# A two-layer hybrid trunk on one core: the first norm as products with a diagonal, and the mixers' modulation pieces loaded earlier

## The chip, the core and the metric

One core of one Trainium2 chip. TensorE (PE) multiplies, VectorE (DVE), ScalarE (ACT) and GpSimd (POOL) work on tiles of 128 partitions, SyncE (SP) issues the loads. The time is the device time of one launch in microseconds; the profile is of one execution. A granted clock of 1.0 is PE at 2.4 GHz, 0.5 is 1.2 GHz.

## The reference

Two layers over 256 tokens of width 1024 in fp32. `mod` is the conditioning of each layer; its six pieces of 1024 shift, scale and gate the two halves of the layer.

```python
def hybrid_layer(x, c, ada_w, ada_b, ...):
    mod = jax.nn.silu(c) @ ada_w + ada_b
    sh_m, sc_m, gt_m, sh_f, sc_f, gt_f = jnp.split(mod, 6)
    h = rms_norm(x, g_pre_mix) * (1.0 + sc_m) + sh_m
    rq, rk, rv, rg, lx, ly, fq, fk, fv, ff, gates = split(h @ w_in)
    y_ret = silu(rg) * head_norm(retention(rope(rq), rope(rk), rv))
    y_lru = gelu(ly) * rg_lru(causal_conv(lx), ...)
    y_fox = forgetting_attention(fq, fk, fv, log_sigmoid(ff + b_f))
    g = sigmoid(gates)
    merged = g[0] * (y_ret @ ret_w_o) + g[1] * (y_lru @ lru_w_o) + g[2] * (y_fox @ fox_w_o)
    x = x + gt_m * rms_norm(merged @ w_out, g_post_mix)
    h = rms_norm(x, g_pre_mlp) * (1.0 + sc_f) + sh_f
    return x + gt_f * rms_norm(square(relu(h @ w1)) @ w2, g_post_mlp)
```

## The kernel before

Every fp32 operand of a large product is split in two: a high half, which ACT casts to the reduced type (line 241), and a low half, which DVE forms as the difference (line 242). A product is then three matmuls (`mm3`, lines 364 to 366): high by high, low by high, high by low. The weights come as 512 KB halves, two for a column block of 256, into `wraw`, a ring of five buffers; SP issues each load when a buffer is free. The split halves stand in `wpair`, four buffers, which are two items. An item is one column block: 48 matmuls of 256 columns into one of two PSUM buffers (`ps`), which DVE and ACT empty: lines 914 (`fql`, low half of the attention's queries), 678 (`fvl`, `fkl`, `yrl`), 872 and 875 (gates and merge).

`mix_order` lists the items of a mixer in the order in which they are computed. In layer 0 the 53 are: 11 for gates and the recurrence's input (`g0`, `lx`, `g1`, `lru`), then `rg` x4, `g1`, `w_r` x4, `g1`, `ly` x4, `fq`, `w_l` x4, `fv` x4, `fq` x3, `fk` x4, `g2` x4, `w_f` x4, `w_o` x4. Layer 1 has 61 with the same 42 at the end.

`weight_order` makes one list, `ORDER`, of all loads. Between the items it puts the modulation's pieces ("ada"): 12 pieces in layer 0's mixer and 8 in layer 1's, spread evenly from the item that is `MIXR[l][0]` items before the mixer's end to the one `MIXR[l][1]` before it. A piece is two loads of 512 KB into `wraw` and, on DVE, two sums `ada_sum` of 128x1024 with the silu of c (`sir`, line 296) and one small addition (line 292); it frees its buffer when the sum is done. `prefetch` walks the list two or three items ahead of the one that PE computes, and each engine works through its own queue in order. `side` puts the pieces of the recurrence, the rotations and the attention between the items by a budget in us per item (`BUDGET`).

The first projection (`first_rows`) is another order. It takes the eight rows k of 128 channels one after the other. A row has four tiles of 512 KB in the pool `wfirst`, later `wraw`: the pieces sc_m and sh_m of that row, the weights of rv, and those of rq and rk. DVE sums the first two, ACT makes the scale `a` and shift `sh` of the row (lines 494, 495), then `hh` (line 513) and its fp32 twin `hf` (line 514), DVE the low half `hl`. PE multiplies the row into all rv, rq and rk banks at once. Before that the rows of x are squared (ACT, line 445), the inverse root comes from POOL (lines 199, 200), DVE scales x to `xn` (line 466), PE transposes it (line 450), ACT copies it to `xr` (line 468). `silu_rows` spreads the silu of c over the partitions (lines 283 to 289).

Of the kernel before, what the change touches and what calls it, by code (L numbers as in the profile page):

```python
# [10 lines left out]
F32 = mybir.dt.float32  # L11
# [22 lines left out]
P = 128  # L34
D = 1024
# [51 lines left out]
    return name in ('rv', 'w_o', 'w2') or (name == 'w1' and cix < 4)  # L87


MIXR = ((22, 8), (20, 8))  # L90
MLPR = ((5, 28), (5, 15))


# [25 lines left out]
def trunk_kernel(ctx, tc, x, c, vec, con, ffw, wts, out):  # L119
# [21 lines left out]
    nc.sync.dma_start(csb[:, :P], con[:, :P])  # L141
    for t in range(2):
        nc.sync.dma_start(xs[:, t, :], x[t])
    nc.sync.dma_start(vsb, vec)

    def cn(name):
        o, w = CON[name]
# [87 lines left out]
    def split_tiles(broad, n=C):  # L235
        return halves_of(wp.tile([P, 2 * D + SLOT_PAD], F32R, name="wpair", tag="wpair", bufs=NHL), broad, PHASE * broad, n)

    def split(t, hi, lo):
        if hi.shape[1] == 2:
            t = t.rearrange("p (k j) c -> p k (j c)", k=2)  # L240
        A.copy(hi, t)  # L241
        V.tensor_tensor(lo, t, hi.bitcast(F32), ALU.subtract)  # L242

    early = []
# [32 lines left out]

    mods = {l: cpool.tile([P, 48], F32, name=f"mod{l}") for l in range(L)}

    def silu_rows():  # L280

        th = sp.tile([P, KD], F32, name="cth", bufs=1)
        A.activation(th, ccol, AF.Tanh, scale=0.5)
        V.scalar_tensor_tensor(th, th, 1.0, ccol, ALU.add, ALU.mult)
        for j, copy in ((0, A.copy), (1, V.tensor_copy)):
            ps = pa.tile([P, 4, P], F32, name="crp", tag="a")
            for k in range(4):
                T.transpose(ps[:, k, :], th[:, 4 * j + k:4 * j + k + 1].to_broadcast([P, P]), ident)
            copy(sir[:, j * 512:(j + 1) * 512], ps.rearrange("p k c -> p (k c)"))

    def mod_bias(l, o, n, src):
        V.tensor_tensor(mods[l][:, o:o + n], src, vc(l, 'ada_b')[:, o:o + n], ALU.add)
# [162 lines left out]
    def first_rows():  # L455


        silu_rows()
        xn = U("T6", [P, 2, D], F32, "xn")
        xr = U("T7", [P, KD, S], F32, "xr")  # L460

        def norm(t):
            ss = sp.tile([P, 1], F32, name="ss1")
            square_sum(xs[:, t, :], ss)
            r = rstd_of(ss, eps)
            V.tensor_scalar(xn[:, t, :], xs[:, t, :], r, None, ALU.mult)
            for k0 in (0, 4):
                transposed(xn[:, t, :], k0, lambda pt, k0: A.copy(xr[:, k0:k0 + 4, t * P:(t + 1) * P], pt))

        one = sp.tile([P, KD], F32, name="one_sc")  # L470
        V.scalar_tensor_tensor(one, vc(0, 'ada_b')[:, 8 * PARTS['sc_m']:8 * PARTS['sc_m'] + 8], 1.0, vc(0, 'pre_mix'),
                               ALU.add, ALU.mult)
        a, sh = mod(0, 'sc_m'), mod(0, 'sh_m')
        hh, hl = new_h()
        raws = []

        def load(n):
            while len(raws) < min(n, 2 * KD):
                home = FIRST[len(raws)]
                if home:  # L480
                    t = U(home, [P, 2, KH * C], F32, "wfirst")
                    for j in range(2):
                        nc.sync.dma_start(t[:, j, :], wts[pos[0], j])
                    raws.append([t[:, j, :].rearrange("p (k c) -> p k c", k=KH) for j in range(2)])
                else:
                    raws.append([raw_half(j) for j in range(2)])
                pos[0] += 1

        def sums(k):
            kc, o = slice(k, k + 1), 8 * PARTS['sh_m'] + k  # L490
            m = sp.tile([P, 2], F32, name="mrow")
            for j in range(2):
                ada_sum(raws[2 * k][j], m[:, j:j + 1])
            A.activation(a[:, kc], m[:, 0:1], AF.Identity, bias=one[:, kc], scale=vc(0, 'pre_mix')[:, kc])
            A.activation(sh[:, kc], m[:, 1:2], AF.Identity, bias=vc(0, 'ada_b')[:, o:o + 1])

        def halves(k, j):
            hi, lo = split_tiles(not j)
            split(raws[2 * k + 1][j], hi, lo)
            return hi, lo  # L500

        load(FIRST_AHEAD)
        norm(0)
        norm(1)
        sums(0)
        rv = [[pool.tile([P, 2, C], F32, name="rvp", tag=tag) for pool, tag in ((pg, "g"), (pz, "z"))]
              for t in range(2)]
        qk = [[pa.tile([P, 2, S], F32, name="qkp", tag="a") for i in range(2)] for j in range(2)]
        for k in range(KD):
            load(2 * k + FIRST_AHEAD + 2)  # L510
            kc, f = slice(k, k + 1), tmp("t1", "hf")[:, 0, :]
            wh, wl = halves(k, 0)
            A.activation(hh[:, k, :], xr[:, k, :], AF.Identity, bias=sh[:, kc], scale=a[:, kc])
            A.activation(f, xr[:, k, :], AF.Identity, bias=sh[:, kc], scale=a[:, kc])
            V.tensor_tensor(hl[:, k, :], f, hh[:, k, :].bitcast(F32), ALU.subtract)
            for j in range(2):
                for t in range(2):
                    tk = slice(t * P, (t + 1) * P)
                    mm3(rv[t][j].rearrange("p h c -> p (h c)"), hh[:, k, tk], hl[:, k, tk], wh[:, j, :], wl[:, j, :],
                        k == 0, k == KD - 1)  # L520
            if k + 1 < KD:
                sums(k + 1)
            wh, wl = halves(k, 1)
            if k == KD - 1:
                nc.sync.dma_start(csb[:, P:5 * P], con[:, P:5 * P])
                early.extend(raw_half(j) for j in range(2))
                nc.sync.dma_start(csb[:, 5 * P:], con[:, 5 * P:])
            for j in range(2):
                for i in range(2):
                    for m in range(2):  # L530
                        n, cs = 2 * j + i, slice(m * P, (m + 1) * P)
                        mm3(qk[j][i][:, m, :], wh[:, n, cs], wl[:, n, cs], hh[:, k, :], hl[:, k, :], k == 0 and m == 0,
                            k == KD - 1 and m == 1, skip_group_check=True)
        return (hh, hl), rv, qk
# [129 lines left out]
    def mixer(l, nm, h=None, rvp=None, qkp=None):  # L664
# [333 lines left out]
        for n, i in mix_order(l):  # L998
# [5 lines left out]
            elif n in ('g0', 'g1', 'g2'):  # L1004
                gate_evac(int(n[1]), i)
            elif n == 'lx':
                if (l, i) == (0, 0):
                    lru_consts()
                conv(i)
            elif n == 'lru':  # L1010
                for h in heads[:NH_R]:
                    finish(h)
                wl.append(weight(l, 'lru', 0))
                gs = [Side(lru_gates(j)) for j in range(4)]
            elif n == 'rg':
                if i == 0:
                    finish(heads[-1])
                    yr = U("T1", [P, KD, S], F32R, "yrh"), U("T2", [P, KD, S], F32R, "yrl")
                ret_gate(i, yr)
            elif n == 'w_r':  # L1020
                if i == 0:
                    rec = Side(recurrence(), *gs)
                merge(0, 'w_r', i, yr)
            elif n == 'ly':
                if i == 0:
                    finish(rec)
                    yl = U("T3", [P, KD, S], F32R, "ylh"), U("T4", [P, KD, S], F32R, "yll")
                gelu_gate(i, yl)
            elif n == 'w_l':
                merge(1, 'w_l', i, yl)  # L1030
            elif n == 'fq':
                if (l, i) == (0, 0):
                    V.tensor_tensor(both, ident[:, 0:NH_F], ident[:, CUM_LO:CUM_LO + NH_F], ALU.add)
                    A.mul(sel, both, -1.0)
                if i == 0:
                    fq = U("T1", [P, NH_F, S], F32R, "fqh"), U("T2", [P, NH_F, S], F32R, "fql")
                fox_q(i, *fq)
            elif n == 'fv':
                if i == 0:
                    fv = U("T3", [P, 2, D], F32R, "fvh"), U("T4", [P, 2, D], F32R, "fvl")  # L1040
                fox_v(i, *fv)
            elif n == 'fk':
                if i == 0:
                    fk = U("T5", [P, NH_F, S], F32R, "fkh", True), U("T6", [P, NH_F, S], F32R, "fkl", True)
                    yf = U("T7", [P, KD, S], F32R, "yfh"), U("T8", [P, KD, S], F32R, "yfl")
                fox_k(i, *fk)
            elif n == 'w_f':
                if i == 0:
                    side()
                    mh, ml = U("T1", [P, KD, S], F32R, "mh"), U("T2", [P, KD, S], F32R, "ml")  # L1050
                    nm = Norms(l, 'm', (l, 'f'), ("T3", "T4", "T7"))
# [168 lines left out]
```

## Time and profile before

| | us |
|---|---|
| three runs, median (lowest, highest) | 1125.44 (1123.99, 1126.6) |
| the profiled execution | 1126.98 |
| its span in the trace | 1125.2 |
| PE busy | 1096.8 (97%) |
| DVE busy | 870.1 (77%) |
| ACT busy | 617.5 (55%) |

Busy time is a sum over all stages. Where PE stands still is read from the table of its waits and from windows laid over single stages, and why, from the timeline of the engine it waits for.

### The profile page before, as it was taken

Reading aid. Unit: us, or ns where it says so; the run is one execution under the profiler, and the core shown is the slowest. Engines: PE = TensorE matmul, PEld = TensorE weight load, DVE = VectorE, ACT = ScalarE, POOL = GpSimd, SP = SyncE. Lnnn points to the kernel's source line nnn. Section 1 sums busy time; section 2 is a strip of 40 time slices with the busy share of each in tenths; the row PEclk is TensorE's granted clock in tenths of the full one; section 3 lists DMA queues with packets and bytes.
Section 4 is the critical chain, followed back from the end, with each engine's and each line's share of the span. In section 5 each row is a group of like instructions: output and inputs, shape, how many; then the busy total and the mean of one; then the engine's idle time right before and its main releaser. Section 6 shows DMA issues by size and latency. Waiting matters only on the chain.

```text
span 1125.2 us, 20478 instructions
## 1 busy us (share of the span) xinstructions
PE 1096.8 (97%) x8164; PEld 1034.8 (92%) x8164; DVE 870.1 (77%) x1324; ACT 617.5 (55%) x924; POOL 43.7 (4%) x60
## 2 busy tenths in 40 slices
PE   6999999999999999999999999999999999999997
PEld 5999999998899889989879999999999997989986
DVE  6998788878887789888586768887868788866543
ACT  6676695544455645444455658755434655645441
POOL 0001000000000210000030010000000002000000
PEclk9999999999999999999999999999999999999999
DMA  9954646679876569998845465566777584875641
GB/s 359 408 179 155 197 136 216 193 248 314 282 249 220 193 214 323 332 327 295 299 140 185 151 194 162 185 207 194 235 248 265 193 290 133 283 269 197 195 159 59
DMA packets 74284, 255.43 MB, mean 227 GB/s; under 512 B 10108, under 2 KB 12492, under 8 KB 74188
## 3 DMA queue, kind: packets, MB, share of 16 engines
q1 hardware_dynamic: 74188, 254.12, 67.2%
q8 instruction: 64, 1.05, 0.4%
q14 instruction: 32, 0.26, 0.1%
HBM read 253.00 MB, written 1.09 MB: 226 GB/s over the span
## 4 chain that ended last, share of the span: by engine, by line
PE 75%; DVE 9%; DMA 8%; issue 4%; ACT 3%; POOL 1%; DVEq 0%; POOLq 0%; SPq 0%; ACTq 0%
PE ps L366 22%; PE ps L365 22%; PE ps L364 22%; DMA wraw<-in_wts_dram 7%; DVE wpair L242 3%; DVE wraw L296 1%; ACT wpair L241 1%; ACT junk L445 1%; PE rvp L364 1%; PE rvp L365 1%; PE rvp L366 1%; POOL rs_v L199 1%; PE qkp L365 1%; PE qkp L364 1%; PE qkp L366 1%
## 5 line engine op out<-in xcount | busy, mean ns | idle before, releaser
L242 DVE TENSOR_TENSOR wpair<-wraw,wpair 128x1024 fp32r<-128x1024 f32 (+1 forms) x286 | 347.3, 1220 | 74.1 <-ACT wpair L241 72.7
L241 ACT CAST wpair<-wraw 128x1024 fp32r<-128x1024 f32 (+1 forms) x286 | 298.3, 1049 | 191.4 <-PE ps L366 122.5
L364 PE MATMUL ps<-hh,wpair 128*128 128x256 f32 x1312 | 364.9, 278 | 5.3 <-DVE fvl L678 2.8
L366 PE MATMUL ps<-hh,wpair 128*128 128x256 f32 x1312 | 363.4, 277 | 0.1
L365 PE MATMUL ps<-hl,wpair 128*128 128x256 f32 x1312 | 363.1, 277 | 0.0
L364 PEld LDWEIGHTS ps<-hh,wpair 128*128 128x128 f32 x1312 | 246.8, 188 | 6.5 <-DVE fvl L678 3.2
L366 PEld LDWEIGHTS ps<-hh,wpair 128*128 128x128 f32 x1312 | 246.5, 188 | 0.4 <-DVE wpair L242 0.3
L365 PEld LDWEIGHTS ps<-hl,wpair 128*128 128x128 f32 x1312 | 246.6, 188 | 0.2
L296 DVE SCALAR_TENSOR_TENSOR wraw<-wraw,sir 128x1024 f32<-128x1024 f32 x82 | 100.0, 1222 | 44.9 <-DMA wraw<-in_wts_dram 44.6
L241 ACT CAST wown<-wraw 128x1024 fp32r<-128x1024 f32 x72 | 74.7, 1048 | 62.4 <-DMA wraw<-in_wts_dram 40.6
L242 DVE TENSOR_TENSOR wown<-wraw,wown 128x1024 fp32r<-128x1024 f32 x72 | 87.4, 1222 | 26.2 <-ACT wown L241 25.9
L364 PE MATMUL ps<-wpair,mih 128*128 128x512 f32 x144 | 56.3, 391 | 0.0
L365 PE MATMUL ps<-wpair,mih 128*128 128x512 f32 x144 | 56.1, 389 | 0.0
L366 PE MATMUL ps<-wpair,mil 128*128 128x512 f32 x144 | 56.0, 389 | 0.0
L364 PE MATMUL ps<-wpair,hh 128*128 128x256 f32 (+1 forms) x144 | 45.6, 317 | 0.0
L365 PE MATMUL ps<-wpair,hh 128*128 128x256 f32 (+1 forms) x144 | 45.4, 316 | 0.0
L366 PE MATMUL ps<-wpair,hl 128*128 128x256 f32 (+1 forms) x144 | 45.4, 315 | 0.0
L364 PE MATMUL ps<-hh,wown 128*128 128x256 f32 x160 | 44.2, 276 | 0.0
L366 PE MATMUL ps<-hh,wown 128*128 128x256 f32 x160 | 44.2, 276 | 0.0
L365 PE MATMUL ps<-hl,wown 128*128 128x256 f32 x160 | 44.2, 276 | 0.0
L364 PE MATMUL ps<-wown,mih 128*128 128x512 f32 x112 | 43.7, 390 | 0.0
L365 PE MATMUL ps<-wown,mih 128*128 128x512 f32 x112 | 43.6, 389 | 0.0
(340 smaller groups left out, 2295.1 us busy)
## 6 DMA issues: line engine op xcount, KB each, us to landing
wraw<-in_wts_dram SPq DMA_DIRECT2D x440, 512.0 KB, 4.4
wfirst<-in_wts_dram SPq DMA_DIRECT2D x28, 512.0 KB, 10.2
rows<-drow SPq DMA_DIRECT2D x10, 512.0 KB, 5.0
xs<-in_x_dram SPq DMA_DIRECT2D x2, 512.0 KB
out_dram<-xs SPq DMA_DIRECT2D x4, 256.0 KB, 2.0
csb<-in_con_dram SPq DMA_DIRECT2D x1, 768.0 KB
csb<-in_con_dram SPq DMA_DIRECT2D x1, 256.0 KB, 10.1
vsb<-in_vec_dram SPq DMA_DIRECT2D x1, 152.0 KB
```

The costliest lines, as they stand in the source:

```text
L199: pin(nc.gpsimd.tensor_scalar(v, part, rest, None, ALU.add))
L241: A.copy(hi, t)
L242: V.tensor_tensor(lo, t, hi.bitcast(F32), ALU.subtract)
L296: V.scalar_tensor_tensor(t, t, 0.5, sir, ALU.mult, ALU.mult, accum_out=m)
L364: T.matmul(ps, ah, bh, start=start, stop=False, **kw)
L365: T.matmul(ps, ah, bl, start=False, stop=False, **kw)
L366: T.matmul(ps, al, bh, start=False, stop=stop, **kw)
L445: return A.activation(j, x, AF.Square, scale=D ** -0.5, accum_out=acc)
```

## The change

The two entries of `MIXR` are raised, so that the modulation pieces stand earlier in `ORDER`. In layer 0 they stood after the items 31 to 36 and 38 to 43 (`fv` to `g2`); now they stand after 17, 18, 20, 22, 24, 26, 28, 29, 31, 33, 35 and 37 (`w_r` to `fk`). In layer 1 the eight move from the items 41 to 51 to the items 29 to 44.

In `first_rows`, DVE no longer scales x and PE no longer transposes it. ACT multiplies the identity by the inverse root (`diag`), and PE forms the scaled and transposed x as fp32 products of x with `diag` (`turned`). The first row's `hh` and `hf` read the product from PSUM; the other rows are copied to `xr` as before. `warm` runs products of a tile of zeros on PE, six before the silu and eight behind it. The copies of `sir` are both on DVE, the first weight's cast is on DVE, an inverse root of eps is made early on POOL, the load of the vectors (`vsb`) comes after the first two weight loads, and `both` and `one_sc` are held to their place in the program.

```diff
-MIXR = ((22, 8), (20, 8))
+MIXR = ((36, 14), (32, 14))
 MLPR = ((5, 28), (5, 15))
...
-    nc.sync.dma_start(vsb, vec)
...
-    def split(t, hi, lo):
+    def split(t, hi, lo, copy=A.copy):
         if hi.shape[1] == 2:
             t = t.rearrange("p (k j) c -> p k (j c)", k=2)
-        A.copy(hi, t)
+        copy(hi, t)
         V.tensor_tensor(lo, t, hi.bitcast(F32), ALU.subtract)
...
+    def warm(n, x):
+
+        ps = pg.tile([P, P], F32, name="warm", tag="g")
+        for i in range(n):
+            T.matmul(ps, lf[:, 0, :], x, start=True, stop=True)
+
     def silu_rows():
 
         th = sp.tile([P, KD], F32, name="cth", bufs=1)
         A.activation(th, ccol, AF.Tanh, scale=0.5)
         V.scalar_tensor_tensor(th, th, 1.0, ccol, ALU.add, ALU.mult)
-        for j, copy in ((0, A.copy), (1, V.tensor_copy)):
+        for j in range(2):
             ps = pa.tile([P, 4, P], F32, name="crp", tag="a")
             for k in range(4):
                 T.transpose(ps[:, k, :], th[:, 4 * j + k:4 * j + k + 1].to_broadcast([P, P]), ident)
-            copy(sir[:, j * 512:(j + 1) * 512], ps.rearrange("p k c -> p (k c)"))
+            V.tensor_copy(sir[:, j * 512:(j + 1) * 512], ps.rearrange("p k c -> p (k c)"))
...
+        rstd_of(eps, eps)
+        warm(6, lf[:, 1, :])
         silu_rows()
-        xn = U("T6", [P, 2, D], F32, "xn")
+        warm(8, sir[:, :P])
         xr = U("T7", [P, KD, S], F32, "xr")
-
-        def norm(t):
+        diag = U("T6", [P, 2, P], F32, "diag")
+        for t in range(2):
             ss = sp.tile([P, 1], F32, name="ss1")
             square_sum(xs[:, t, :], ss)
-            r = rstd_of(ss, eps)
-            V.tensor_scalar(xn[:, t, :], xs[:, t, :], r, None, ALU.mult)
-            for k0 in (0, 4):
-                transposed(xn[:, t, :], k0, lambda pt, k0: A.copy(xr[:, k0:k0 + 4, t * P:(t + 1) * P], pt))
-
-        one = sp.tile([P, KD], F32, name="one_sc")
-        V.scalar_tensor_tensor(one, vc(0, 'ada_b')[:, 8 * PARTS['sc_m']:8 * PARTS['sc_m'] + 8], 1.0, vc(0, 'pre_mix'),
-                               ALU.add, ALU.mult)
+            A.mul(diag[:, t, :], ident, rstd_of(ss, eps, tc.keep_in_program_order))
+
+        def turned(k0):
+
+            pt = pa.tile([P, 2, 2, P], F32, name="xT", tag="a")
+            for k in range(2):
+                for t in range(2):
+                    T.matmul(pt[:, k, t, :], xs[:, t, (k0 + k) * P:(k0 + k + 1) * P], diag[:, t, :],
+                             start=k == t == 0, stop=k == t == 1, skip_group_check=True)
+            return pt.rearrange("p k t c -> p k (t c)")
+
...
-        def sums(k):
-            kc, o = slice(k, k + 1), 8 * PARTS['sh_m'] + k
+        def row_sums(k):
             m = sp.tile([P, 2], F32, name="mrow")
             for j in range(2):
                 ada_sum(raws[2 * k][j], m[:, j:j + 1])
+            return m
+
+        def sums(k, m):
+            kc, o = slice(k, k + 1), 8 * PARTS['sh_m'] + k
             A.activation(a[:, kc], m[:, 0:1], AF.Identity, bias=one[:, kc], scale=vc(0, 'pre_mix')[:, kc])
             A.activation(sh[:, kc], m[:, 1:2], AF.Identity, bias=vc(0, 'ada_b')[:, o:o + 1])
 
-        def halves(k, j):
+        def halves(k, j, copy=A.copy):
             hi, lo = split_tiles(not j)
-            split(raws[2 * k + 1][j], hi, lo)
+            split(raws[2 * k + 1][j], hi, lo, copy)
             return hi, lo
 
+        load(1)
+        nc.sync.dma_start(vsb, vec)
         load(FIRST_AHEAD)
-        norm(0)
-        norm(1)
-        sums(0)
+        m = row_sums(0)
+        one = sp.tile([P, KD], F32, name="one_sc")
+        tc.keep_in_program_order(V.scalar_tensor_tensor(
+            one, vc(0, 'ada_b')[:, 8 * PARTS['sc_m']:8 * PARTS['sc_m'] + 8], 1.0, vc(0, 'pre_mix'), ALU.add, ALU.mult))
+        sums(0, m)
+        xT = [turned(0)]
         rv = [[pool.tile([P, 2, C], F32, name="rvp", tag=tag) for pool, tag in ((pg, "g"), (pz, "z"))]
               for t in range(2)]
-        qk = [[pa.tile([P, 2, S], F32, name="qkp", tag="a") for i in range(2)] for j in range(2)]
         for k in range(KD):
             load(2 * k + FIRST_AHEAD + 2)
             kc, f = slice(k, k + 1), tmp("t1", "hf")[:, 0, :]
-            wh, wl = halves(k, 0)
-            A.activation(hh[:, k, :], xr[:, k, :], AF.Identity, bias=sh[:, kc], scale=a[:, kc])
-            A.activation(f, xr[:, k, :], AF.Identity, bias=sh[:, kc], scale=a[:, kc])
+            wh, wl = halves(k, 0, A.copy if k else V.tensor_copy)
+            xk = xr[:, k, :] if k else xT[0][:, 0, :]
+            A.activation(hh[:, k, :], xk, AF.Identity, bias=sh[:, kc], scale=a[:, kc])
+            A.activation(f, xk, AF.Identity, bias=sh[:, kc], scale=a[:, kc])
+            if k == 0:
+                A.copy(xr[:, 1, :], xT[0][:, 1, :])
+                for k0 in (2, 4, 6):
+                    A.copy(xr[:, k0:k0 + 2, :], turned(k0))
+                qk = [[pa.tile([P, 2, S], F32, name="qkp", tag="a") for i in range(2)] for j in range(2)]
...
-                sums(k + 1)
+                sums(k + 1, row_sums(k + 1))
...
-                    V.tensor_tensor(both, ident[:, 0:NH_F], ident[:, CUM_LO:CUM_LO + NH_F], ALU.add)
+                    tc.keep_in_program_order(V.tensor_tensor(both, ident[:, 0:NH_F], ident[:, CUM_LO:CUM_LO + NH_F], ALU.add))
```

On ACT, at the start of the program, the rows before (`sir` is the silu of c, `junk` the squares, `xT` the transposed x in PSUM, `wpair` the split weights, `mod` the scale and shift):

```order
L289 COPY sir<-crp 128x512
L445 ACTIVATE junk,ss_170<-xs 128x1024
L445 ACTIVATE junk,ss_190<-xs 128x1024
L468 COPY xr<-xT 128x4x128
L494 ACTIVATE mod_111<-mrow,one_sc,vsb 128x1
L468 COPY xr<-xT 128x4x128
L495 ACTIVATE mod_111<-mrow,vsb 128x1
L468 COPY xr<-xT 128x4x128 x2
L241 CAST wpair<-wfirst 128x2x512
L513 ACTIVATE hh<-xr,mod_111 128x256
L514 ACTIVATE hf<-xr,mod_111 128x256
```

and now:

```order
L450 ACTIVATE junk,ss_153<-xs 128x1024
L450 ACTIVATE junk,ss_161<-xs 128x1024
L472 ACTIVATE diag<-csb,rs_r 128x128 x2
L536 COPY xr<-xT 128x512
L508 ACTIVATE mod_110<-mrow,vsb 128x1
L507 ACTIVATE mod_110<-mrow,one_sc,vsb 128x1
L536 COPY xr<-xT 128x512
L531 ACTIVATE hh<-xT,mod_110 128x256
L532 ACTIVATE hf<-xT,mod_110 128x256
L534 COPY xr<-xT 128x256
L536 COPY xr<-xT 128x512
L240 CAST wpair<-wfirst 128x4x256
```

The first weight's cast is gone from between the copies and `hh`; behind `hf` stand two copies, and then the cast of the qk tile. `diag` stands behind the squares.

On DVE, in layer 0's items w_r (`gate` empties their PSUM, `lru_*` is the recurrence), before:

```order
L872 SCALAR_TENSOR_TENSOR gate<-gate,ps 128x512
L723 SCALAR_TENSOR_TENSOR lru_t<-lru_a,lru_t 128x512 x2
L725 TENSOR_TENSOR lru_u<-lru_u,lru_t 128x512
L242 TENSOR_TENSOR wpair<-wraw,wpair 128x4x256
L728 SCALAR_TENSOR_TENSOR lru_u<-lru_a,lru_u 128x256 x2
L725 TENSOR_TENSOR lru_u<-lru_u,lru_t 128x512
L872 SCALAR_TENSOR_TENSOR gate<-gate,ps 128x512
L728 SCALAR_TENSOR_TENSOR lru_u<-lru_a,lru_u 128x256
L242 TENSOR_TENSOR wpair<-wraw,wpair 128x4x256 x2
L728 SCALAR_TENSOR_TENSOR lru_u<-lru_a,lru_u 128x256
L723 SCALAR_TENSOR_TENSOR lru_t<-lru_a,lru_t 128x512
L242 TENSOR_TENSOR wpair<-wraw,wpair 128x4x256
```

and now, some rows on in the same part:

```order
L746 SCALAR_TENSOR_TENSOR lru_t<-lru_a,lru_t 128x512
L301 SCALAR_TENSOR_TENSOR wraw,mcol<-wraw,sir 128x1024
L748 TENSOR_TENSOR lru_u<-lru_u,lru_t 128x512
L895 SCALAR_TENSOR_TENSOR gate<-gate,ps 128x512
L751 SCALAR_TENSOR_TENSOR lru_u<-lru_a,lru_u 128x256
L301 SCALAR_TENSOR_TENSOR wraw,mcol<-wraw,sir 128x1024
L241 TENSOR_TENSOR wpair<-wraw,wpair 128x4x256
L297 TENSOR_TENSOR mod_110<-mcol,vsb 128x2
L241 TENSOR_TENSOR wpair<-wraw,wpair 128x4x256
L751 SCALAR_TENSOR_TENSOR lru_u<-lru_a,lru_u 128x256
L241 TENSOR_TENSOR wpair<-wraw,wpair 128x4x256
L301 SCALAR_TENSOR_TENSOR wraw,mcol<-wraw,sir 128x1024 x2
```

Modulation sums (`mcol`) stand now between the low halves and the scans; before there were none here.

On DVE, in layer 0's attention (`sm` is the softmax, `fkl` the low half of the keys), before:

```order
L292 TENSOR_TENSOR mod_111<-mcol,vsb 128x2
L296 SCALAR_TENSOR_TENSOR wraw,mcol<-wraw,sir 128x1024
L961 TENSOR_SCALAR mx<-mx 128x2
L966 RECIPROCAL sm__3569<-sm__3569 128x2
L296 SCALAR_TENSOR_TENSOR wraw,mcol<-wraw,sir 128x1024
L967 TENSOR_SCALAR sm<-sm,sm__3569 128x128
L968 TENSOR_SCALAR sm<-sm,sm__3569 128x256
L966 RECIPROCAL sm__3586<-sm__3586 128x2
L242 TENSOR_TENSOR wpair<-wraw,wpair 128x4x256
L967 TENSOR_SCALAR sm<-sm,sm__3586 128x128
L968 TENSOR_SCALAR sm<-sm,sm__3586 128x256
L678 TENSOR_TENSOR fkl<-ps,fkh 128x512
```

and now:

```order
L984 TENSOR_SCALAR mx<-mx 128x2
L989 RECIPROCAL sm__3621<-sm__3621 128x2
L990 TENSOR_SCALAR sm<-sm,sm__3621 128x128
L991 TENSOR_SCALAR sm<-sm,sm__3621 128x256
L989 RECIPROCAL sm__3638<-sm__3638 128x2
L990 TENSOR_SCALAR sm<-sm,sm__3638 128x128
L991 TENSOR_SCALAR sm<-sm,sm__3638 128x256
L241 TENSOR_TENSOR wpair<-wraw,wpair 128x4x256
L701 TENSOR_TENSOR fkl<-ps,fkh 128x512
L241 TENSOR_TENSOR wpair<-wraw,wpair 128x4x256 x2
L701 TENSOR_TENSOR fkl<-ps,fkh 128x512
L241 TENSOR_TENSOR wpair<-wraw,wpair 128x4x256
```

The sums ahead of the softmax's last scalings and of `fkl` are gone.

## Rows read from the trace of the kernel before

**Rows 1.** Page, busy time of PE over the span (us, share, instructions).
```profile
PE 1096.8 (97%) x8164; PEld 1034.8 (92%) x8164; DVE 870.1 (77%) x1324; ACT 617.5 (55%) x924; POOL 43.7 (4%) x60
```

**Rows 2.** PE's waits: total us, times, longest us.
```profile
PE xT L450 <- DVE xn L466: 3.6, 1, 3.6
PE ps L364 <- DVE fvl L678: 2.8, 2, 1.5
PE rvp L364 <- ACT hh L513: 2.3, 1, 2.3
...
PE ps L364 <- DVE fql L914: 2.0, 1, 2.0
```

**Rows 3.** Windows: length, busy us by engine (PE, PEld, DVE, ACT, POOL), clock, DMA share, GB/s.
```profile
157.50:211.00 53.50, 53.37 (x471) 53.34 (x471) 45.85 (x60) 35.45 (x46) 0.00 (x0) 1.00 0.58 186
240.00:275.00 35.00, 32.24 (x276) 31.84 (x275) 30.01 (x63) 13.09 (x18) 0.00 (x0) 1.00 0.89 301
299.00:340.00 41.00, 38.64 (x319) 37.91 (x318) 35.75 (x102) 22.61 (x54) 0.00 (x0) 0.96 0.76 255
800.00:875.00 75.00, 72.21 (x617) 71.19 (x616) 59.29 (x124) 34.55 (x56) 0.00 (x0) 1.00 0.78 259
309.00:314.00 5.00, 5.00 (x31) 5.00 (x32) 4.52 (x7) 1.81 (x3) 0.00 (x0) 0.66 0.81 251
16.50:19.50 3.00, 3.00 (x9) 2.33 (x8) 3.00 (x6) 2.15 (x3) 0.00 (x0) 0.50 1.02 408
```

**Rows 4.** Timeline of DVE at layer 1's fq: start, duration, engine, line, operation, wait.
```profile
829.24 1.23 DVE L296 SCALAR_TENSOR_TENSOR wraw<-wraw,sir 128x1024 f32<-128x1024 f32 x1 [3.81 <-DMA wraw<-in_wts_dram]
...
830.39 1.22 DVE L242 TENSOR_TENSOR wpair<-wraw,wpair 128x1024 fp32r<-128x1024 f32 x1
831.53 1.22 DVE L296 SCALAR_TENSOR_TENSOR wraw<-wraw,sir 128x1024 f32<-128x1024 f32 x1
...
832.67 0.68 DVE L914 SCALAR_TENSOR_TENSOR fql<-ps,fqh 128x512 fp32r<-128x512 f32 x1
833.27 1.21 DVE L242 TENSOR_TENSOR wpair<-wraw,wpair 128x1024 fp32r<-128x1024 f32 x1
```

**Rows 5.** Groups by line and shape: the modulation sums on DVE.
```profile
L296 DVE SCALAR_TENSOR_TENSOR wraw<-wraw,sir 128x1024 f32<-128x1024 f32 x82 | 100.0, 1222 | 44.9 <-DMA wraw<-in_wts_dram 44.6
```

**Rows 6.** Timeline of PE at the start.
```profile
10.19 3.52 PE L450 MATMUL xT<-csb,xn 128*128 128x128 f32 x16 [3.60 <-DVE xn L466]
16.03 0.50 PE L364 MATMUL rvp<-wpair,hh 128*128 128x512 f32 x1 [2.33 <-ACT hh L513]
...
28.66 0.63 PE L364 MATMUL rvp<-wpair,hh 128*128 128x512 f32 x2
```

**Rows 7.** Timeline of ACT at the start.
```profile
14.42 1.05 ACT L241 CAST wpair<-wfirst 128x1024 fp32r<-128x1024 f32 x1
15.37 0.61 ACT L513 ACTIVATE hh<-xr,mod 128x256 fp32r<-128x256 f32 x1
...
16.36 1.03 ACT L241 CAST wpair<-wfirst 128x1024 fp32r<-128x1024 f32 x1
```

**Rows 8.** Timeline of DVE at the start.
```profile
9.38 1.58 DVE L466 TENSOR_SCALAR xn<-xs,rs_r 128x1024 f32<-128x1024 f32 x2 [1.80 <-POOL rs_r L200]
```

**Rows 9.** DMA issues around 3.6 to 3.95 us: count, size, us to landing.
```profile
wfirst<-in_wts_dram SPq DMA_DIRECT2D x1, 512.0 KB, 6.9
```

**Rows 10.** Timeline of PE, fp32 products with `csb` at 275 us.
```profile
275.22 0.59 PE L803 MATMUL pc<-csb,lf 128*128 128x256 f32 x2
275.65 0.38 PE L804 MATMUL pc<-csb,lf 128*128 128x128 f32 x2
```

**Rows 11.** Timeline of DVE, 157 us (y of retention) and 222 to 228 (w_l).
```profile
157.53 0.68 DVE L678 TENSOR_TENSOR yrl<-th,yrh 128x512 fp32r<-128x512 f32 x1
...
222.27 0.69 DVE L875 SCALAR_TENSOR_TENSOR mt<-gate,ps 128x512 f32<-128x512 f32 x1 [0.36 <-PE ps L366]
...
227.71 0.69 DVE L875 SCALAR_TENSOR_TENSOR mt<-gate,ps 128x512 f32<-128x512 f32 x1 [0.41 <-PE ps L366]
```

## The prediction

> **What bounds the kernel now.** I read the busy shares first: TensorE (PE) works 97% of the span [rows 1], so a gain can only come from where it stands still, some 28 us, or runs at half clock. The table of PE's waits names the places the change touches [rows 2]: 3.6 us for the scaled rows of the first norm, 2.33 us for the first `hh`, 2.8 us for the low halves `fvl`, 2.0 us for one `fql`. The windows then say what the stretches lose [rows 3]: 240 to 275 us (layer 0's fv and fq items) holds 32.24 us of PE work, 2.76 idle; 299 to 340 (the attention) 38.64, 2.36 idle; 800 to 875 (the same zone of layer 1) 72.21, 2.79 idle. In 309 to 314 the granted clock is 0.66, of which 1.0 is 2.4 GHz: (1 - 0.66) x 5 = 1.7 us more. Layer 0's rg to w_l stretch, 157.5 to 211, idles PE by 0.13 only, and VectorE (DVE) is busy 45.85 of 53.5 there.
>
> The DVE timeline shows how a stall is made [rows 4]. DVE works in order. At 829.24 the modulation sum (line 296) has waited 3.81 us for its load; a low half and a second sum follow, and `fql`, whose PSUM buffer PE needs, begins at 832.67. `ps` has two buffers, so a late evacuation stops the next gemm. All 82 such sums together waited 44.9 us, nearly all for a DMA: 0.55 each [rows 5].
>
> **Start, part by part.** The profiled execution took 1126.98 us, of which 1125.2 is its span; the median of three runs is 1125.44, so it stands 1.54 above it. The sum is made against 1126.98.
>
> Before, PE begins the 16 transposes at 10.19, is done 3.52 later, waits 2.33 for `hh`, starts the first product at 16.03 and the third round (of the eight of 5.46 us) at 28.66 [rows 6]. On ScalarE (ACT), the cast of the first weight starts at 14.42, `hh` at 15.37, the cast of the qk tile at 16.36 [rows 7]. DVE starts the two scalings at 9.38 for 1.58 [rows 8].
> Removed: those scalings. The sums then start when the first load lands. The second load was issued about 3.5 and took 6.9 to land [rows 9], so 10.4; loads land about 1.3 apart, and both lose the issue of `vsb` ahead of them (about 0.4): 8.7 and 10.0. So the sums run 8.7 to 9.9 and 10.1 to 11.3, and `sh` and `a` are ready at 11.7 (an operation of ACT on one column after the last sum).
> Added on PE: 16 fp32 products. A 128-column fp32 product is half of the 256-column pair's 0.43 [rows 10], 0.215, the same as the transposes' 3.52 / 16 = 0.22; after `diag` (about 9.3: the scalings began at 9.38 behind the same roots) they end by about 12.3 and hide behind the sums. `hh` comes after one PSUM copy, at 12.5, and the first product at about 13.2, 2.8 us earlier. The products with zeros fill waits; PE has nothing else there, so I price them at 0 (bounds 0 and, should they overrun into the transposition, 0.5).
> But this 2.8 doesn't last. Behind `hh` ACT now has `hf` and two copies before the cast of qk (14.4 against 16.36), and DVE does that tile's low half (15.5 to 16.7) before both sums of round 1 (1.15 each, to 19.0), which `a`, `sh`, the next cast (19.4 to 20.4) and `hh` follow: round 1 starts about 20.9, the third at 26.9. That is 1.7 earlier, and stays so: DVE needs less per round than PE's 5.46.
> The clock decides the other end. At 16.5 to 19.5 it was 0.50 [rows 3], 1.2 GHz, right after the 2.33 us wait [rows 2]. The new start has no such wait: case A, 2.4 GHz kept, -1.7. Case B, the products with the diagonal at 1.2 GHz (0.43 each) and the first round too: `hh` at 14.5, third round at 28.25, -0.4. A worse start is worth up to +0.5. I take -1.3, A weighing 70%.
> The Trainium skill ("TensorE: Matmul & The Clock Gate", What's actually happening) holds that the throttled state is the default and activity releases it; by that, B would be the case unless the products with zeros count as activity, and the start would give 0.4. The trace speaks for A: the old transposes ran at the full-clock price of 0.22 after 3.6 us without work [rows 2, 6].
> Vector's cast, the early rstd, the moved `vsb` load, `both` and `one_sc` cost DVE or a queue under 1 us each where it waited anyway: 0.
>
> **Middle: the pieces moved ahead.** The work is the same; only its place changes. In layer 0 twelve pieces (24 loads, 24 sums of 1.15, from 829.24 to 830.39 in [rows 4], 12 small additions) are loaded among the items w_r to fk instead of fv to g2; in layer 1 eight likewise.
> Removed: in layer 0 the 2.76 idle and the 2.36 idle with 1.7 of clock, and 0.3 between (275 to 299): 7.1. In layer 1: 2.8.
> Added in layer 0: DVE load. Between `yrl` (157.53 [rows 11]) and the first low half of ly's first item the new order has 6 sums x 1.15 = 6.9; 9 low halves x 1.14 (830.39 to 831.53 [rows 4]) = 10.3; 23 operations of 512 columns or scans x 0.60 (832.67 to 833.27) = 13.8; 4 tensor-scalars x about 0.37 (half of a scaling's 0.75 [rows 8]) = 1.5: 32.5. From 158.1 that is 190.6, with two waits for ACT of 0.3 each 191.2. PE wants that half at 189.5: w_l's first two evacuations are at 222.27 and 227.71 [rows 11], 5.45 an item, and the first of them ends six items after ly begins. So 1.7 late, bounds 0 (half a microsecond less on four operations hides it) and 3.5.
> After that DVE is nearly full until about 246, with 2 to 3.5 us of slack from the two `ps` and two weight pairs. Its waits for loads come on top, and eat the slack: bounds 0 and 5, I take 1.5, because the demand falls from 3.71 to 3.09 loads per item, 356 to 297 GB/s (0.512 MB each, 5.45 us), and 301 GB/s was got in 240 to 275 [rows 3]. Where DVE now sees 5 sums around layer 1's fq it sees 2; no sum is left behind fq's last evacuations. The attention keeps 0.3.
> Added in layer 1: its recurrence ends earlier and DVE has idle time there, so +0.8 (bounds 0 and 4).
> Sum: -1.3 - 7.1 - 2.8 + 1.7 + 1.5 + 0.3 + 0.8 = -6.9, so 1126.98 - 6.9 = 1120.1, and against the median 1118.5.
>
> **Rivals.**
> 1. The stalls only move. ly and w_l get them in place of fv and fq: the first lag at 3.5 and the second at 5 leave -6.9 + 1.8 + 3.5 = -1.6, and with layer 1 halfway to its 4 the change is zero: 1123.8 to 1125.4. For it: DVE has no idle time left there. Against: the load demand falls. 0.20.
> 2. All lag is hidden: -1.7 - 9.9 + 0.3 = -11.3, 1114.1. For it: two `ps` and prefetch of two items cover 1.7 us. Against: DVE at 97% must make up the lag from waits it doesn't have. 0.17.
> 3. Slower. Each sum again stands at DVE's head for its load, now where DVE has no idle time to absorb it: 24 x 0.55 = 13.2 [rows 5] + 1.7 - 2.5 slack = 12.4 in layer 0, 16 x 0.55 = 8.8 less some 6 that DVE's idle time there takes up, 2.8, in layer 1, against -11.2 removed: +4, 1129.4. It decides once the new stalls pass 11.2 us. For it: the loads wait for buffers which DVE itself frees, so a late DVE makes late loads. Against: these waits had been where 3.71 loads per item were asked. 0.08.
> The moves might also do nothing of what they say, if the planner's budget put the sums back behind the evacuations; the new order shows otherwise.
>
> **How the numbers follow.** Forecast 0.55 (own range 1115 to 1121.5), rivals 0.20, 0.17, 0.08. The range of 8 in 10 goes from 1113 to 1124.5: it leaves out the slow rival and the worse half of the first. What can be told from no change is 0.2%, 2.25 us: 1123.2 to 1127.7. Faster: 0.55 + 0.17 + a quarter of the first rival = 0.77; same: the rest of it, less a little = 0.14; slower 0.09.
>
> **What would show it.** The start: first product near 13.2 at clock 1.0, third round near 26.9. The middle: no idle PE over 1 us in the fv, fq and attention zones of either layer, clock 1.0 all through the attention. The price: a PE wait of 1 to 3 us near the first ly items, for a low half of a weight pair. Wrong, if the table of PE's waits shows over 8 us for `wpair` or `gate`, if sums still wait 0.5 us each, or if 300 to 340 keeps its half clock.

## The result and the profile after

The changed kernel takes 1132.38 us (median of eight runs, 1130.19 to 1138.25), the kernel before 1124.72 (eight runs): ratio 1.0073, 95% interval 1.0059 to 1.0087. It is slower by 8 us where 7 us less had been forecast. Its profiled execution, 1138.25 us, was the slowest of the eight; a second profile of it, told of below, took 1128.86.

PE's waits after, from the table of waits (total us, times, longest us), beside [rows 2]:

```profile
PE ps L371 <- DVE wpair L241: 5.8, 5, 2.1
PE ps L369 <- DVE fvl L701: 3.6, 1, 3.6
PE xT L479 <- ACT diag L472: 2.9, 2, 2.5
PE rvp L369 <- ACT hh L531: 1.8, 3, 1.4
```

The two waits of the start are still there, shorter. The two `fvl` waits of before (2.8 us together) were in layer 0 and are gone; the one of 3.6 us stands in layer 1, between 800 and 875 us, where there was none. A new wait leads: 5.8 us for low halves of weights (`wpair`), 3.5 of them between 157 and 240 us and 2.3 between 735 and 800. The windows, with the columns of [rows 3], first two of before that are not shown there:

```profile
157.00:240.00 83.00, 82.87 (x730) 82.67 (x729) 69.00 (x88) 49.71 (x62) 0.00 (x0) 1.00 0.61 192
735.00:800.00 65.00, 65.00 (x572) 65.00 (x572) 50.24 (x62) 34.42 (x41) 0.00 (x0) 1.00 0.64 203
```

and after:

```profile
157.00:240.00 83.00, 77.36 (x649) 75.78 (x649) 76.65 (x114) 46.44 (x62) 0.00 (x0) 0.98 0.75 249
240.00:275.00 35.00, 35.00 (x304) 35.00 (x303) 31.41 (x63) 15.81 (x20) 0.00 (x0) 1.00 0.87 296
299.00:340.00 41.00, 40.95 (x358) 40.75 (x357) 28.10 (x75) 22.86 (x49) 0.00 (x0) 1.00 0.47 153
735.00:800.00 65.00, 61.64 (x531) 60.55 (x530) 54.61 (x79) 31.34 (x37) 0.00 (x0) 1.00 0.75 243
800.00:875.00 75.00, 70.74 (x587) 70.27 (x586) 53.43 (x100) 32.67 (x48) 0.00 (x0) 0.95 0.67 227
```

240 to 275 and 299 to 340 lost 2.76 and 2.36 us of PE and some clock before; now they lose 0.00 and 0.05 at full clock. 157 to 240 lost 0.13, now 5.6, at a granted clock of 0.98 ((1 - 0.98) x 83 = 1.7 us more). In layer 1 PE was busy for 65.00 us of 735 to 800 before and loses 3.4 now, and 800 to 875 loses 4.3 at 0.95 ((1 - 0.95) x 75 = 3.75 us more), where it lost 2.8 at 1.00. So layer 0's loss of some 7 us has moved, and layer 1's has grown from 2.8 to 11 us. The sums as one group, beside [rows 5]:

```profile
L301 DVE SCALAR_TENSOR_TENSOR wraw<-wraw,sir 128x1024 f32<-128x1024 f32 x82 | 100.1, 1221 | 44.4 <-DMA wraw<-in_wts_dram 43.5 <-DVE wraw L301 0.4
```

The modulation sums still wait 44.4 us for their loads (44.9 before). Only 40 of the 82 were moved, 24 in layer 0 and 16 in layer 1. These as groups, layer 0 and then layer 1, before:

```profile
L296 DVE SCALAR_TENSOR_TENSOR wraw<-wraw,sir 128x1024 f32<-128x1024 f32 x24 | 29.3, 1222 | 12.3 <-DMA wraw<-in_wts_dram 12.2
L296 DVE SCALAR_TENSOR_TENSOR wraw<-wraw,sir 128x1024 f32<-128x1024 f32 x16 | 19.5, 1222 | 14.7 <-DMA wraw<-in_wts_dram 14.6
```

and after:

```profile
L301 DVE SCALAR_TENSOR_TENSOR wraw<-wraw,sir 128x1024 f32<-128x1024 f32 x24 | 29.3, 1220 | 10.3 <-DMA wraw<-in_wts_dram 10.3
L301 DVE SCALAR_TENSOR_TENSOR wraw<-wraw,sir 128x1024 f32<-128x1024 f32 x16 | 19.5, 1221 | 17.5 <-DMA wraw<-in_wts_dram 17.5
```

The moved sums wait 27.8 us in all, as long as at their old places (27.0). One such wait, on DVE's timeline at layer 1's first ly items (start, duration, engine, line, operation, wait):

```profile
746.67 1.21 DVE L241 TENSOR_TENSOR wpair<-wraw,wpair 128x1024 fp32r<-128x1024 f32 x1
751.92 1.23 DVE L301 SCALAR_TENSOR_TENSOR wraw<-wraw,sir 128x1024 f32<-128x1024 f32 x1 [4.04 <-DMA wraw<-in_wts_dram]
...
753.76 1.23 DVE L301 SCALAR_TENSOR_TENSOR wraw<-wraw,sir 128x1024 f32<-128x1024 f32 x1 [0.60 <-DMA wraw<-in_wts_dram]
...
754.91 1.22 DVE L241 TENSOR_TENSOR wpair<-wraw,wpair 128x1024 fp32r<-128x1024 f32 x1
```

DVE stands 4.04 us before the first sum. ACT had cast a weight half well before, and PE waits for its low half:

```profile
746.25 1.04 ACT L240 CAST wpair<-wraw 128x1024 fp32r<-128x1024 f32 x1
```

```profile
756.19 0.38 PE L371 MATMUL ps<-hh,wpair 128*128 128x256 f32 x1 [2.09 <-DVE wpair L241]
```

The cast ended at 747.3, so its low half was ready to be formed then; it begins at 754.91, behind both sums, and PE stood 2.09 us for it. Why the sum's load came late is on SP's side, in the line that issues loads, for the one instruction at 746.7:

```profile
L216 SPq DMA_DIRECT2D wraw<-in_wts_dram x1: 328/328/328, 746.7 to 746.7; - x1
...
  DVE wraw L301: 4.0, 1
...
DMA to landing us min/median/max: 5.1/5.1/5.1
```

SP issued it at 746.7, just when the low half before (745.46 to 746.7) had freed a buffer of `wraw`. It landed 5.1 us later, and the sum waited 4.0 of these. By the count of issues and casts, two of the five buffers served the two sums; the other three held weight halves, whose low halves DVE forms behind these sums and so can't free before.

The start of this execution, on GpSimd (the second row's root), PE and in a window:

```profile
7.76 1.38 POOL L198 TENSOR_SCALAR rs_v<-ss,eps 128x1 f32<-128x1 f32 x1 [0.47 <-ACT junk L450]
9.22 1.48 POOL L199 TENSOR_TENSOR rs_r<-rs_v,mhalf 128x1 f32<-128x1 f32 x1
```

```profile
11.19 1.23 PE L479 MATMUL xT<-diag,xs 128*128 128x128 f32 x4 [2.47 <-ACT diag L472]
```

```profile
29.92 0.50 PE L369 MATMUL rvp<-wpair,hh 128*128 128x512 f32 x1 [0.16 <-ACT hh L531]
```

```profile
11.00:14.00 3.00, 2.81 (x13) 2.81 (x14) 1.65 (x2) 0.14 (x1) 0.00 (x0) 0.52 1.03 415
```

GpSimd's two operations on the second root took 1.38 and 1.48 us, PE stood 2.47 for `diag` and ran the products at 0.52, about 1.2 GHz, and the third round began at 29.92 against 28.66 before [rows 6].

### The profile page after: what moved, and what is told of

It is laid out like the page before. It is cut to its first block, busy times and chain, and to the rows that moved or that the text cites. A ratio compares the mean times of both kernels' runs of the same rounds, so it can differ in the third digit from the quotient of the medians.

```text
span 1136.5 us, 20566 instructions
## 1 busy us (share of the span) xinstructions
PE 1106.1 (97%) x8208; PEld 1043.5 (92%) x8208; DVE 871.3 (77%) x1324; ACT 616.4 (54%) x924; POOL 48.8 (4%) x62
## 4 chain that ended last, share of the span: by engine, by line
PE 68%; DVE 16%; DMA 6%; ACT 5%; issue 4%; POOL 1%; SPq 0%; DVEq 0%; POOLq 0%; ACTq 0%
PE ps L371 20%; PE ps L370 20%; PE ps L369 20%; DVE wpair L241 6%; DMA wraw<-in_wts_dram 4%; ACT wpair L240 2%; DVE wraw L301 2%; POOL rs_v L198 1%; DVE lru_u L751 1%; POOL rs_r L199 1%; DMA rows<-drow 1%; ACT junk L450 1%; PE rvp L369 1%; PE rvp L370 0%; PE qkp L370 0%
## 5 line engine op out<-in xcount | busy, mean ns | idle before, releaser
L301 DVE SCALAR_TENSOR_TENSOR wraw<-wraw,sir 128x1024 f32<-128x1024 f32 x82 | 100.1, 1221 | 44.4 <-DMA wraw<-in_wts_dram 43.5
L241 DVE TENSOR_TENSOR wown<-wraw,wown 128x1024 fp32r<-128x1024 f32 x72 | 87.5, 1222 | 26.9 <-ACT wown L240 26.5
L369 PE MATMUL ps<-wpair,hh 128*128 128x256 f32 (+1 forms) x144 | 47.0, 326 | 3.6 <-DVE fvl L701 3.6
L370 PE MATMUL ps<-wpair,hh 128*128 128x256 f32 (+1 forms) x144 | 46.8, 325 | 0.7 <-DVE wpair L241 0.7
L369 PE MATMUL ps<-wown,mih 128*128 128x512 f32 x112 | 43.7, 390 | 0.0
L371 PE MATMUL ps<-wown,mil 128*128 128x512 f32 x112 | 43.6, 389 | 0.0
```

The lines of the kernel that those rows point to most:

```text
L301: V.scalar_tensor_tensor(t, t, 0.5, sir, ALU.mult, ALU.mult, accum_out=m)
L369: T.matmul(ps, ah, bh, start=start, stop=False, **kw)
L370: T.matmul(ps, ah, bl, start=False, stop=False, **kw)
L371: T.matmul(ps, al, bh, start=False, stop=stop, **kw)
```

## The experiments

All times are medians, ratios are against the kernel before on the same chip. "In load order" means the following edit, which holds each sum on DVE behind the low half that was loaded just before it; without it the planner's order stands, in which a sum can come ahead of low halves that were loaded earlier.

```diff
-        V.tensor_tensor(lo, t, hi.bitcast(F32), ALU.subtract)
+        low.append(V.tensor_tensor(lo, t, hi.bitcast(F32), ALU.subtract).ins)
...
-            ada_sum(raw_half(j), m[:, j:j + 1])
+            t = raw_half(j)
+            with tc.issue_after(low[-1]):
+                ada_sum(t, m[:, j:j + 1])
```

**The two parts apart.** The kernel before with the new places alone:

```diff
-MIXR = ((22, 8), (20, 8))
+MIXR = ((36, 14), (32, 14))
```

> The kernel before with the new MIXR and nothing else. Theory (both parts lose, the pieces most of it): of the 7.7 us by which the changed kernel is slower the pieces make about 6, so some 1130.5 us, with PE waits for low halves (wpair) and fvl of 9 to 13 us in all between 157 and 240 us and 735 and 825 us, and the sums on DVE still waiting about 0.5 us each for their loads. Rival 1 (the new start makes the loss, the pieces are even): 1124 to 1126. Rival 2 (the forecast's middle was right, -5.6): 1119.

1131.77 us, ratio 1.0060 (1.0041 to 1.0078). The theory held: the pieces make most of the loss. And the changed kernel with the old places:

```diff
-MIXR = ((36, 14), (32, 14))
+MIXR = ((22, 8), (20, 8))
```

> The changed kernel with the old MIXR: only the new start. Theory: the third round of the first projection begins near 29.9 us as in the changed kernel, 1.3 later than before, because GpSimd's operations on the second row's root take 1.4 and 1.5 us instead of 0.3 and 0.6 while DVE sums beside them, and PE falls to half clock in the 2.5 us wait: about 1126. Rival 1 (the start gains as forecast, 1.3): 1123.4. Rival 2 (the start makes the whole loss): 1132.

1122.73 us, ratio 0.9983 (0.9970 to 0.9997): the start gains about 2 us. My theory, that the start loses, fell; rival 1 held. In this profile GpSimd's second operation is long too,

```profile
8.57 1.38 POOL L199 TENSOR_TENSOR rs_r<-rs_v,mhalf 128x1 f32<-128x1 f32 x1
```

but the first is not (0.30 us), PE's products with `diag` run at full clock, and the third round begins at 27.64, before the 28.66 of the old start. So the collision comes in more than one execution; here it leaves the start 1.0 us of its gain, where in the first profile it took all of it.

**Load order.** The changed kernel with the edit above.

> The changed kernel, with each modulation sum held on DVE behind the low half that was loaded before it (load order instead of the planner's). Theory (a sum stands at DVE's head for a load that was issued only 5 us earlier, ahead of low halves that are ready and for which PE waits): the PE waits for wpair and fvl between 157 and 240 us and 735 and 825 us fall from 13 us to under 4, the half-clock stretches there go, and the time falls by 7 to 12 us, to 1120 to 1125. Rival (DVE has simply too much to do in these stretches): the same DVE work, so waits within 3 us of the changed kernel's, 1130 to 1134.

1117.15 us, ratio 0.9931 (0.9912 to 0.9950). The cause held; the time is below the theory's range, since the fall is 15 us where 7 to 12 were expected. The sums as a group, and the windows (columns as above):

```profile
L302 DVE SCALAR_TENSOR_TENSOR wraw<-wraw,sir 128x1024 f32<-128x1024 f32 x82 | 98.2, 1222 | 1.1 <-DMA wraw<-in_wts_dram 1.0
```

```profile
157.00:240.00 83.00, 79.74 (x689) 78.56 (x688) 77.72 (x118) 44.62 (x56) 0.00 (x0) 1.00 0.77 259
240.00:345.00 105.00, 104.83 (x908) 104.35 (x907) 80.16 (x167) 55.79 (x99) 0.00 (x0) 1.00 0.67 221
735.00:800.00 65.00, 65.00 (x571) 65.00 (x570) 60.43 (x92) 34.89 (x44) 0.00 (x0) 1.00 0.87 288
800.00:875.00 75.00, 75.00 (x656) 74.94 (x656) 52.52 (x109) 39.59 (x69) 0.00 (x0) 1.00 0.63 207
```

The same 82 sums with the same busy time wait 1.1 us instead of 44.4. In layer 1, PE is busy for all of 735 to 875, while DVE does no less there than in the changed kernel (60.43 + 52.52 against 54.61 + 53.43) and more loads come through in 735 to 800 (288 against 243 GB/s). Nor do the loads land sooner. The issues of 735 to 800 (count, size, median us to landing), in the changed kernel and then in load order:

```profile
wraw<-in_wts_dram SPq DMA_DIRECT2D x31, 512.0 KB, 4.4
wraw<-in_wts_dram SPq DMA_DIRECT2D x36, 512.0 KB, 5.3
```

So neither DVE's load nor the DMA set the stalls of layer 1: the order did. In layer 0, 157 to 240 still loses 3.3 us, with DVE busy for 77.72 of 83.

**The roots first.** The changed kernel, with the first sums behind the second root:

```diff
-            A.mul(diag[:, t, :], ident, rstd_of(ss, eps, tc.keep_in_program_order))
+            r = rstd_of(ss, eps, tc.keep_in_program_order)
+            A.mul(diag[:, t, :], ident, r)
+        seen = V.tensor_copy(sp.tile([P, 1], F32, name="seen"), r).ins
...
-        m = row_sums(0)
+        with tc.issue_after(seen):
+            m = row_sums(0)
```

> The changed kernel, with the first two sums on DVE held until the second row's root is done, by a copy of that root of one column on DVE. Theory (GpSimd is slowed by DVE's sums beside it): the operations on the second root take 0.3 and 0.6 us again, the second diag begins near 8.7 instead of 10.73, the products follow at full clock, and the third round begins near 27.2 instead of 29.9: 2 to 3 us less, 1129.5 to 1130.5. Rival (GpSimd is slow there for another reason): root as late as before, the sums later still, third round at 30 or later, 1132 to 1134.

1132.11 us, ratio 1.0061 (1.0043 to 1.0079): no gain. The mechanism is there, on GpSimd's timeline:

```profile
8.28 0.30 POOL L198 TENSOR_SCALAR rs_v<-ss,eps 128x1 f32<-128x1 f32 x1 [0.33 <-ACT junk L450]
8.66 0.57 POOL L199 TENSOR_TENSOR rs_r<-rs_v,mhalf 128x1 f32<-128x1 f32 x1
```

Both operations on the second root are short again, and the third round began at 27.82. But the median stays where it was (1132.38), so the collision is no cause of the result.

**Each layer alone.** The kernel before with the new places in one layer.

```diff
-MIXR = ((22, 8), (20, 8))
+MIXR = ((36, 14), (20, 8))
```

> The kernel before with the new place of the pieces in layer 0 alone. Theory: what layer 0 loses in the w_r to w_l items (5 us with some half clock) is about what it saves in fv, fq and the attention (7 us): 1123 to 1126. Rival (layer 0 makes the loss): 1129 to 1132.

1123.74 us, ratio 0.9990 (0.9979 to 1.0002).

```diff
-MIXR = ((22, 8), (20, 8))
+MIXR = ((22, 8), (32, 14))
```

> The kernel before with the new place of the pieces in layer 1 alone. Theory: layer 1, where before only 2.8 us were lost, now waits 6 to 8 us for wpair and fvl between 735 and 835 us, with half clock behind it: 1128 to 1132, nearly the whole loss. Rival (layer 0 makes the loss): 1124 to 1126.

1133.06 us (1127.72 to 1133.64), ratio 1.0060 (1.0043 to 1.0076). Both theories held in kind, the second 1 us above its range: layer 0 is about even, layer 1 makes the loss. Their windows, layer 0's and then layer 1's:

```profile
157.00:240.00 83.00, 78.47 (x680) 77.31 (x679) 77.34 (x115) 45.20 (x59) 0.00 (x0) 1.00 0.77 258
240.00:345.00 105.00, 104.01 (x892) 102.79 (x892) 78.79 (x168) 54.76 (x97) 0.00 (x0) 1.00 0.64 219
```

```profile
735.00:800.00 65.00, 62.01 (x530) 60.84 (x529) 52.08 (x74) 32.08 (x39) 0.00 (x0) 1.00 0.76 252
800.00:875.00 75.00, 72.10 (x610) 71.64 (x609) 53.22 (x106) 34.38 (x56) 0.00 (x0) 0.98 0.63 218
```

Layer 0 pays 4.5 us in 157 to 240 for the 5.1 that it had lost in 240 to 275 and 299 to 340 [rows 3] (1.0 is left in 240 to 345). Layer 1 pays 3.0 in 735 to 800 and 2.9 in 800 to 875, at a lower clock; the 2.9 are new waits, 2.1 of them for `fvl`. Its profiled execution (1127.72) was the fastest of the six, so these windows show less than the median's loss. A sum on DVE's timeline there waits as in the changed kernel:

```profile
744.24 1.22 DVE L296 SCALAR_TENSOR_TENSOR wraw<-wraw,sir 128x1024 f32<-128x1024 f32 x1 [4.08 <-DMA wraw<-in_wts_dram]
```

**Load order at the old places.** First the kernel before with the load-order edit alone.

> The kernel before (old start, old MIXR), with each modulation sum held on DVE behind the low half loaded before it. Theory (the order of the sums on DVE makes the stalls, wherever the pieces stand): the waits of the sums fall from 44.9 us to under 5, the waits for fvl, fql and sm (7 us) with the half clock at 310 us go, and the time falls by 6 to 9 us, to 1116 to 1119. Rival (the stalls of before came of five loads' worth of DVE work around fq, whatever the order): 1122 to 1125, waits of fvl and fql as before.

1115.40 us, ratio 0.9909 (0.9896 to 0.9923), a little better than the theory's range. The sums wait 1.9 us:

```profile
L297 DVE SCALAR_TENSOR_TENSOR wraw<-wraw,sir 128x1024 f32<-128x1024 f32 x82 | 98.2, 1219 | 1.9 <-DMA wraw<-in_wts_dram 1.7
```

Then the changed kernel with the old places and the edit: the new start and the load order, without the move of the pieces.

> The changed kernel with the old MIXR and each modulation sum held on DVE behind the low half loaded before it. Theory: as the kernel before with the load order, and the start's 2 us less: 1114 to 1117, no slower than the changed kernel in load order (1117.15), whose layer 0 still waits 3.3 us between 157 and 240 us for wpair. Rival (in load order the earlier places are the better ones, since fewer sums stand around fq): 1118 to 1121.

1111.09 us, ratio 0.9875 (0.9863 to 0.9888), better than the theory's range and 13.9 us below the kernel before (1124.98 in that comparison). The windows:

```profile
157.00:240.00 83.00, 83.00 (x732) 83.00 (x732) 68.50 (x85) 48.44 (x60) 0.00 (x0) 1.00 0.56 188
240.00:345.00 105.00, 104.83 (x910) 104.35 (x909) 93.62 (x206) 54.50 (x99) 0.00 (x0) 1.00 0.83 292
735.00:800.00 65.00, 65.00 (x570) 65.00 (x569) 51.62 (x76) 33.70 (x43) 0.00 (x0) 1.00 0.59 200
800.00:875.00 75.00, 74.95 (x654) 74.69 (x653) 63.27 (x141) 39.90 (x75) 0.00 (x0) 1.00 0.78 272
```

PE loses 0.22 us in all four together. In load order the old places are the better ones: 1111.09 against 1117.15. Of the 6 us that the new places still cost, 3.3 are seen in layer 0's w_r to w_l items, where DVE has most to do; the rest was not found.

**The zeros.** The same kernel without both calls of `warm`:

```diff
-        warm(6, lf[:, 1, :])
...
-        warm(8, sir[:, :P])
```

> The changed kernel with the old MIXR and the sums in load order (1111.09 us), without the products with zeros (both calls of warm). Theory (a wait of PE of 2.3 us and more before the first products is followed by half clock in part of the executions, and the zeros close such a wait between the silu's transposes and the products with diag): some of its runs at the level of 1111, others 1.5 to 3 us above; median 1111.5 to 1114. Rival (the zeros change nothing, the shorter chain does): 1110.5 to 1111.5 in all runs.

1110.64 us (1110.03 to 1113.52), ratio 0.9880 (0.9862 to 0.9899): four of five runs at or below the kernel with the zeros. The theory predicted slower ones for part of the runs; there was one, the profiled, in which PE stood 5.8 us for `diag`:

```profile
PE xT L480 <- ACT diag L473: 5.8, 2, 3.4
```

In that execution GpSimd's operations on the second root were long too (1.37 and 1.50 us), so its slowness is not shown to come of the missing zeros. The rival is nearer: the zeros bring nothing to the median.

**The roots first, again,** on the load-ordered kernel, with the edit shown above.

> The changed kernel with the old MIXR and the sums in load order (1111.09 us), with the first two sums on DVE held behind the second row's root. Theory (GpSimd is only slowed in executions in which the first load lands before 8 us, and the holding costs a sum's start otherwise): 1110.5 to 1112, second root's two operations 0.3 and 0.6 us. Rival (the collision costs most executions over a microsecond): 1108 to 1110.

1111.24 us, ratio 0.9882 (0.9864 to 0.9901): the same as without, as the theory said.

**The changed kernel once more,** unedited.

> The changed kernel itself, for a second profile (the first was its slowest run, 1138.25 against a median of 1132.38). Theory: some 1131 to 1133; the sums again wait 40 to 48 us in all, PE again waits 5 to 8 us for wpair and 2 to 4 for fvl; the third round of the start between 26.6 and 28 us, and GpSimd's second root slow only if the first sum begins before it.

1128.86 us in its one run, below the range I gave. PE's waits and the start:

```profile
PE ps L371 <- DVE wpair L241: 4.4, 3, 2.3
PE ps L369 <- DVE fvl L701: 3.8, 3, 2.6
```

```profile
13.06 0.50 PE L369 MATMUL rvp<-wpair,hh 128*128 128x512 f32 x1 [0.48 <-ACT hh L531]
```

```profile
26.55 0.73 PE L369 MATMUL rvp<-wpair,hh 128*128 128x512 f32 x2 [0.24 <-ACT hh L531]
```

The stalls are of the same kind; `wpair` is 1.4 us below the first profile and below the 5 to 8 expected, and the sums wait 46.4 us. The start is the forecast's, without collision and without half clock.

## Why the prediction was wrong

**The start: right in its times, its worth in the changed kernel not shown.** The first product was put at 13.2 and the third round at 26.9; the second profile has 13.06 and 26.55. The worth, -1.3 forecast, is -1.9 by the ratio of the start alone (0.3 to 3.4 by its interval). Case A held there. But with the pieces moved no gain is seen: the pieces alone measured 1.0060, pieces and start together 1.0073, with intervals that overlap. What the forecast missed is that this start has its own bad executions: where the first sum begins beside the second root, GpSimd's operations take 1.4 and 1.5 us, and the third round moves to 29.92. The Trainium skill ("SBUF — State Buffer", SBUF: two separate sides) says that VectorE and GpSimd share a port pair which the one that starts first holds for its whole instruction, and that an operation of VectorE with two SBUF inputs counts against a GpSimd operation that reads SBUF. The traces agree in the lengths: 1.38 and 1.48 us beside sums of 1.22, against 0.30 and 0.57 with the sums behind. The records don't settle who starts first: a GpSimd operation that began 0.07 us before a sum took 1.38 us (7.76 against 7.83, first profile), and one that began 0.09 us before a sum took 0.30 us (8.20 against 8.29, the start alone). The prediction had no term for this, and the median shows no price.

**The removed stalls: right in layer 0.** The 7.1 us of layer 0 went: 240 to 275 and 299 to 340 are full, at full clock, in the first profile (1.0 us is left in 240 to 345 with layer 0 alone). In layer 1 the old stall for `fql` (2.0 us) went as well, but 800 to 875 loses as much as before or more, to a new one for `fvl`: 3.6 us and 2.6 in the two profiles.

**The new stalls: the step that failed.** The prediction priced what DVE's waits for loads would cost as small, 1.5 in layer 0 "because the demand falls from 3.71 to 3.09 loads per item", and 0.8 for all new stalls of layer 1. (Its rates, 356 and 297 GB/s, go with loads of 0.524 MB, which is 512 KB, and not with the 0.512 that it names.) The runs show that demand doesn't set the waits. The sums wait 44.4 us with the pieces at the new places as at the old (44.9), with fewer loads per item: the 24 moved ones of layer 0 10.3 for 12.3, the 16 of layer 1 17.5 for 14.7. In load order, with the same demand, all 82 wait 1.1 us and the 40 moved ones not at all. One of the prediction's own signs of being wrong came with it: the sums still wait 0.5 us each. What sets them is the place of the sum in DVE's queue: ahead of low halves loaded earlier, so that DVE holds up the buffers that the ring needs for the sum's own load. The prediction had read that mechanism from [rows 4] and then priced it as a matter of bandwidth.

In numbers: for layer 0 it forecast -7.1 + 3.5 = -3.6, and the layer alone measured -1.1 (interval -2.4 to +0.2). For layer 1 it forecast -2.8 + 0.8 = -2.0, and the layer alone measured +6.8 by its ratio (+4.8 to +8.5). The second is 8.8 us of an error of 15 (forecast -6.9, measured +8.2 by the ratio), the first 2.5. The start alone did 0.6 better than forecast. The parts measured alone add up to +3.8, so some 4 us of the error stand in no part alone, and where they come from is open. The argument for layer 1 was that DVE has idle time there to absorb the sums. But a sum that waits at the head of DVE's queue blocks the ready work behind it, so much of DVE's idle time is such waiting and can absorb no sum: beside the 17.5 us of it in layer 1, PE stands still for 7.6.

**The rivals.** The third, each sum again at DVE's head for its load, at 0.08, was the mechanism. Its time of 1129.4 was near, but partly by luck, since by its place it was wrong: it put 12.4 us into layer 0 and 2.8 into layer 1. The bound of 4 us for layer 1's new stalls was too small: the changed kernel has 7.6 us of idle in 735 to 875 and a lower clock behind it.

**Open.** At the old places the start is worth 2 us in the planner's order and 4.3 us in load order (1115.40 to 1111.09). One wait of 0.94 us for the attention's low half in the load-ordered kernel before is a part; the rest was not traced, as its one profiled execution was its fastest. It was also not tried whether holding the sums back by any other amount does as well as load order.

## What to carry to other kernels

An operation that waits for its own load should stand in its engine's queue behind all work whose data was loaded earlier; a planner's order can put it ahead, and with a ring of buffers one late load can then hold up DVE and PE together, as it did here. Before moving such operations, test their order: here an edit of a few lines that fixes it gave about 10 us where moving them lost 7. The wait seen here at the head of a queue could not be priced by the mean bandwidth; it went by how long before the need the load could be issued, and by what stood behind it in the queue.

## What the runs showed of the hardware

- A load of 512 KB took 5.1 us from issue to landing (746.7 to 751.8) while the queue moved 288 GB/s, the rate that load order has as the mean of 735 to 800. There the loads took 5.3 us in the median, longer than in the changed kernel (4.4), and no sum waited: the wait went by the place in DVE's queue.
- GpSimd's additions and powers on one column took 0.30 and 0.57 us without DVE's sums beside them and 1.38 and 1.48 us with them.
- PE's products with zeros before the first real work made no difference that the medians show (1111.09 with, 1110.64 without).
